# One column sum for the variance of two layer norms, and two transposed groups in the small PSUM ring, in a two-layer decoder trunk

## The chip, the cores and the metric

One core of a Trainium2 chip runs the whole kernel in one launch. The metric is the device time of that launch in microseconds (us), as the median of several executions.

## The reference, cut to what matters

The input is one sequence of 512 positions with 1024 features. Two layers follow each other. Layer 0 mixes with a state-space group and a stick-breaking attention group, layer 1 with a gated causal convolution of width 31 that has a layer norm of its own. Each layer adds its mixer to the scaled residual, normalises, adds a squared-ReLU MLP of width 4096, and normalises again:

```python
def layer_norm(x, g, b):
    mu = jnp.mean(xf, axis=-1, keepdims=True)
    var = jnp.mean(jnp.square(xf - mu), axis=-1, keepdims=True)
    y = (xf - mu) * lax.rsqrt(var + LN_EPS)
    return y * g + b

for layer in range(2):
    mix = ... if layer % 2 == 0 else conformer_conv(x, ...)
    x = layer_norm(DEEPNORM_ALPHA * x + mix, ln1_g[layer], ln1_b[layer])
    ffn = jnp.square(jax.nn.relu(x @ w1 + b1)) @ w2 + b2
    x = layer_norm(DEEPNORM_ALPHA * x + ffn, ln2_g[layer], ln2_b[layer])
```

So there are four layer norms between the stages and one inside the convolution. The kernel calls them a (after the mixer of layer 0), b (after the MLP of layer 0), c (inside the convolution), d (after the mixer of layer 1), and the last one, which works on another layout.

## The kernel before

**Layout.** Activations stand with features on the 128 partitions and positions along the free dimension: eight tiles X[0] to X[7] of 128 features by 512 positions. A matrix product in full precision is made of three products of rounded parts: a number is split into a high part (`whi`, `xh`, `hh`, `ah`) by ScalarE and the rest (`wlo`, `xl`, `hl`, `al`) by VectorE, and TensorE adds high by high, high by low and low by high into one PSUM bank (`gemm`, L257).

**Layer norm in this layout.** The mean over the features is a sum over the partitions, so it is a product on TensorE with a constant matrix `ones` that holds 1/1024. It runs for each half of the positions (256 columns) apart. `LN.add` keeps a running sum of the eight tiles on VectorE, and `LN.colmean` makes the mean of it with one product (the tile `mp`). `LN.centre` then subtracts the mean from each of the eight tiles on VectorE and squares each on ScalarE (the tiles `sq`), and adds the squares in four pairs on VectorE. It returns four tiles, and `LN.scale` makes the variance with four products that add into one bank (the tile `vp`), all on line L955. After that ScalarE takes an inverse root, VectorE refines it (the helpers on L386 and L390), and `ln_to_x` scales each tile and splits it into high and low parts for the next stage. The intermediate tiles of 128x512 come from a ring `tmp` of eight.

**What covers a layer norm.** TensorE works its queue in order. `tail_norm_lead` puts the last product of a stage and the first product of the next around each norm: `Tail.run(n)` makes n output tiles of the stage that ends (`tlb`, `tld`: 24 matmuls of 256 columns each), `Lead.run(n)` makes n tiles of the next stage for the first half of the positions (`pl` for the convolution's input, `fl` for the MLP of layer 1). `BEFORE = (1, 3, 1, 2)` says how many of them stand before the mean and before the variance of the first half, and of the second half. `issue_after` ties the norm's products behind them. For norm b the lead holds four tiles, of which one is left after the variance of the second half; for norm d it holds six, of which three are left.

**PSUM.** After the mixer two rings share the eight banks: `nps` with six (the tag "n"), and `stp` with two (the tag "st"), which the norms' products use, and later the MLP of layer 1 for its hidden tiles.

**The residual of layer 1.** The MLP of layer 1 makes its output with positions on the partitions, so `residual()` scales X and turns it: 32 transposes of 128x128 on TensorE, in eight groups of four, each group into one bank (`xt`, L1343), and each bank copied back to X by ScalarE (L1346). All eight groups took `nps` banks. At that point six tiles of the lead `fl` hold the six banks of the ring until ScalarE has taken their ReLU (the tile `r`), in `pair`, which also squares them and makes their sums and splits (`q`, `ah`, `al`, L1363 and L1364). After the residual `seven` starts the second product (`s`, L1397), whose banks come from the same ring.

**Order.** Within these bounds a planner orders the instructions of each engine when the program is built: the one that was written first goes first, and another goes ahead where by the planner's own clock the first is not ready yet. On the chip each engine then keeps its list in that order. For the convolution alone the order on TensorE, VectorE and ScalarE is written out by hand (`CONV_ORDER`).

Of the kernel before, what the change touches and what calls it, by code (L numbers as in the profile page):

```python
# [13 lines left out]
ALU = mybir.AluOpType  # L14
# [29 lines left out]
LEAD = 6  # L44
TOGETHER = {'fl1': 2}
LN_ON_V = "abcd"
KEEP_FROM = 8
AHEAD = (5, 4)
FJ = 3
# [110 lines left out]
def units_of(name, w, k0, nk, cols, width):  # L160

    ncol = 1024 // nk
    out = []
    for c in cols:
        base = c // width * width
        src = w[k0 * P : (k0 + nk) * P, base : base + width].rearrange("(k p) n -> p k n", p=P)
        out.append(((name, k0, base), src, nk, ncol, c - base, width))
    return out
# [29 lines left out]
def kernel(ctx: ExitStack, tc: tile.TileContext, a: dict, out: bass.AP):  # L198
# [42 lines left out]
    def pv(n, i):  # L241
        if n == "mix_b_in":
            return PB[:, i : i + 1]
        return PV[:, vrow[n] + i : vrow[n] + i + 1]
# [67 lines left out]
    with tc.high_priority():  # L312
        for j in range(KT):
            tag, bufs = (("spt", MIX_BUFS[3]), ("wt", MIX_BUFS[4]), ("q", QK_BUFS[0]), ("k", QK_BUFS[1]))[(0, 1, 0, 1, 0, 1, 3, 2)[j]]
            xt = att.tile([P, 4, P], F32, tag=tag, name=f"xin{j}", bufs=bufs)
# [69 lines left out]
    def tt(o, x, y, op):  # L385
        V.tensor_tensor(o, x, y, op=op)  # L386
        return o
# [244 lines left out]
    def in_proj(tile_i, name):  # L632
        w = W.next()
        ps = mm(name)
        proj_last[:] = [gemm(ps, w, slice(0, P), xs, 0, T)]
        return ps, pv("mix_b_in", tile_i)

    Ud = [tc.dram_tile([P, T], F32, name=f"Ud{j}") for j in range(4)]
    for j in range(4):
        ps, b = in_proj(j, f"u{j}") if j else (u0, pv("mix_b_in", 0))  # L640
# [231 lines left out]
    def nps(name):  # L872
        return nps_.tile([P, T], F32, tag="n", name=name)
# [7 lines left out]
    def tmp(name, dt=F32):  # L881
        return hid.tile([P, T], dt, tag="tmp", name=name, bufs=8)
# [14 lines left out]
    for layer in range(2):  # L897
# [4 lines left out]
        for nb in FFN_BLOCKS[layer]:  # L902
# [11 lines left out]
            for m in range(k0, k0 + nb, 4):  # L914
                units += units_of("f10", a["ffn_w1"][0], 0, 8, range(m * P, min(m + 4, k0 + nb) * P, 128), 256)
                if m >= KEEP_FROM:
                    keep_at["f", m + 3] = kept[n : n + 2]
# [14 lines left out]
    class LN:  # L932
# [29 lines left out]
        def centre(self, ys, c0, c1, other=None):  # L962

            mu = self.colmean([self.s[c0]], c0, c1, "m", other)
            sq = []
            for j, y in enumerate(ys):
                tt(y[:, c0:c1], y[:, c0:c1], mu, ALU.subtract)
                sq.append(tmp(f"sq{self.n}{c0}{j}")[:, c0:c1])
                act(sq[j], y[:, c0:c1], AF.Square)
            for j in range(0, KT, 2):  # L970
                tt(sq[j], sq[j], sq[j + 1], ALU.add)
            return sq[::2]

        def scale(self, sq, c0, c1, other=None):
            var = self.colmean(sq, c0, c1, "v", other)
# [360 lines left out]
    def residual():  # L1336
        for j in range(KT):
            act(X[j], X[j], AF.Identity, bias=rb[3][:, j : j + 1], scale=ALPHA)
        for f in range(2):
            pss = [nps(f"xt{b}{f}") for b in range(4)]  # L1340
            for b in range(4):
                for i in range(4):
                    PE.transpose(pss[b][:, i * P : (i + 1) * P], X[4 * f + i][:, b * P : (b + 1) * P], ident)  # L1343
            for b in range(4):
                XT[2 * b + f] = X[4 * f + b]
                S.copy(X[4 * f + b], pss[b])  # L1346
# [64 lines left out]
    for bi, nb in enumerate(FFN_BLOCKS[1][:-1]):  # L1411
        if bi:
            W.load_quads(k0, a["ffn_w2"][1], k0, nb)
        As = [pair(m, first[m : m + 2] if bi == 0 else None) for m in range(k0, k0 + nb, 2)]
        if bi == 0:
            residual()
        seven(k0, As, bi == 0)
        k0 += nb
# [26 lines left out]
    pss = [nps(f"h{b}0") for b in range(4)]  # L1445
# [66 lines left out]
```

## Time and profile before

| | |
|---|---|
| median of 3 runs | 1172.3 us (1169.31 to 1175.33) |
| the profiled execution | 1168.87 us, of which the span from first to last instruction is 1167.2 us |
| TensorE busy in the span | 1137.1 us (97%), mean granted clock 0.997 |
| VectorE, ScalarE, GpSimd busy | 816.3 us (70%), 550.0 us (47%), 66.2 us (6%) |
| DMA | 169.59 MB, mean 145 GB/s |

The rows that follow in the prediction come from views of this one execution. In a row of the timeline stand the start and the length in us, the engine, the line, the operation, the output and the inputs, the shape and how many were merged; in brackets the engine's idle time ahead of it and what ended that. A row of the chain of waits has start, length, engine, tile and line. Matmuls overlap: their listed length is longer than the distance from one to the next, so distances between starts are used. One matmul of plain f32 numbers, as on L955, shows as two records, each with its own weight load; the rows count the records.

### The profile page before, as it was taken

Reading aid. Unit: us, or ns where it says so; the run is one execution under the profiler, and the core shown is the slowest. Engines: PE = TensorE matmul, PEld = TensorE weight load, DVE = VectorE, ACT = ScalarE, POOL = GpSimd, SP = SyncE. Lnnn points to the kernel's source line nnn. Section 1 sums busy time; section 2 is a strip of 40 time slices with the busy share of each in tenths; the row PEclk is TensorE's granted clock in tenths of the full one; section 3 lists DMA queues with packets and bytes.
Section 4 is the critical chain, followed back from the end, with each engine's and each line's share of the span. In section 5 each row is a group of like instructions: output and inputs, shape, how many; then the busy total and the mean of one; then the engine's idle time right before and its main releaser. Section 6 shows DMA issues by size and latency. Waiting matters only on the chain.

```text
span 1167.2 us, 17873 instructions
## 1 busy us (share of the span) xinstructions
PE 1137.1 (97%) x7180; PEld 952.1 (82%) x7180; DVE 816.3 (70%) x1389; ACT 550.0 (47%) x838; POOL 66.2 (6%) x125
## 2 busy tenths in 40 slices
PE   9989999999999999999999999899999999999997
PEld 7777777799888888888899877589988888888885
DVE  7999875498645545645647699987595958688337
ACT  6857779345525424424413132463663536263530
POOL 1021211000000000000011211002000000000000
PEclk9999999999999999999999999999999999999999
DMA  8621221242687877888435743246024151515211
GB/s 204 167 66 50 72 69 62 90 146 69 225 286 254 284 275 270 270 281 276 147 116 174 252 143 112 72 149 216 1 82 136 38 161 45 170 30 162 63 54 72
DMA packets 145907, 169.59 MB, mean 145 GB/s; under 512 B 13922, under 2 KB 119138, under 8 KB 145824
## 3 DMA queue, kind: packets, MB, share of 16 engines
q1 hardware_dynamic: 137024, 136.96, 37.1%
q0 software_dynamic: 8640, 31.46, 8.0%
q8 instruction: 56, 0.92, 0.3%
q14 instruction: 27, 0.22, 0.1%
q10 hardware_dynamic: 160, 0.03, 0.0%
HBM read 132.12 MB, written 35.65 MB: 144 GB/s over the span
## 4 chain that ended last, share of the span: by engine, by line
PE 78%; ACT 4%; DMA 3%; DVE 2%; issue 1%; POOL 0%; SPq 0%; DVEq 0%; ACTq 0%
PE f L257 21%; PE acf L257 10%; PE s L1397 10%; PE fl L257 5%; PE tld L257 4%; PE h L1442 4%; PE tlb L257 4%; PE pv L257 3%; DMA raw<-in_ffn_w_dram 3%; PE pg L257 3%; PE cw L1171 3%; PE tla L257 2%; PE acmo L257 2%; PE pl L257 2%; PE gg L257 1%
## 5 line engine op out<-in xcount | busy, mean ns | idle before, releaser
L111 ACT CAST whi<-raw 128x1024 fp32r<-128x1024 f32 (+1 forms) x150 | 156.7, 1061 | 259.9 <-PE acf L257 67.3
L112 DVE TENSOR_TENSOR wlo<-raw,whi 128x1024 fp32r<-128x1024 f32 (+1 forms) x150 | 183.7, 1238 | 122.9 <-ACT whi L111 120.6
L257 PE MATMUL f<-xah,whi 128*128 128x512 f32 x208 | 81.0, 390 | 0.0
L257 PE MATMUL f<-xal,whi 128*128 128x512 f32 x208 | 81.0, 389 | 0.0
L257 PE MATMUL f<-xah,wlo 128*128 128x512 f32 x208 | 80.9, 389 | 0.0
L257 PE MATMUL f<-xdh,whi 128*128 128x512 f32 x208 | 80.9, 389 | 0.0
L257 PE MATMUL f<-xdl,whi 128*128 128x512 f32 x208 | 80.9, 389 | 0.0
L257 PE MATMUL f<-xdh,wlo 128*128 128x512 f32 x208 | 80.9, 389 | 0.0
L257 PE MATMUL acf<-hh,wlo 128*128 128x512 f32 x192 | 75.7, 394 | 0.0
L257 PE MATMUL acf<-hl,whi 128*128 128x512 f32 x192 | 75.7, 394 | 0.0
L257 PE MATMUL acf<-hh,whi 128*128 128x512 f32 x192 | 75.3, 392 | 0.0
L1397 PE MATMUL s<-whi,ah 128*128 128x512 f32 x168 | 64.6, 392 | 0.6 <-ACT X L1346 0.6
L1397 PE MATMUL s<-whi,al 128*128 128x512 f32 x168 | 65.0, 390 | 0.0
L1397 PE MATMUL s<-wlo,ah 128*128 128x512 f32 x168 | 64.9, 389 | 0.0
L112 DVE TENSOR_TENSOR wlo<-quad,whi 128x1536 fp32r<-128x1536 f32 x28 | 49.2, 1756 | 8.6 <-ACT whi L111 8.5
L390 DVE SCALAR_TENSOR_TENSOR cy<-hp,wdw,cy 128x512 f32<-128x512 f32 (+1 forms) x75 | 49.6, 661 | 1.3 <-ACT cy L186 1.3
L111 ACT CAST whi<-quad 128x1536 fp32r<-128x1536 f32 x28 | 41.1, 1478 | 19.4 <-PE s L1397 9.5
L96 POOL DMA_DIRECT2D whi<-kepth x30 | 16.0, 535 | 551.8 <-PE tlb L257 388.3
L257 PEld LDWEIGHTS f<-xdh,wlo 128*128 128x128 f32 x208 | 39.0, 188 | 8.2
L257 PEld LDWEIGHTS f<-xal,whi 128*128 128x128 f32 x208 | 39.0, 188 | 8.1
L257 PEld LDWEIGHTS f<-xah,wlo 128*128 128x128 f32 x208 | 39.0, 188 | 8.1
L257 PEld LDWEIGHTS f<-xdl,whi 128*128 128x128 f32 x208 | 39.0, 188 | 8.1
(647 smaller groups left out, 3061.4 us busy)
## 6 DMA issues: line engine op xcount, KB each, us to landing
raw<-in_ffn_w_dram SPq DMA_DIRECT2D x35, 1024.0 KB, 5.6
kepth<-whi SPq DMA_DIRECT2D x30, 512.0 KB, 3.9
keptl<-wlo SPq DMA_DIRECT2D x30, 512.0 KB, 9.4
whi<-kepth POOLq DMA_DIRECT2D x30, 512.0 KB, 3.5
wlo<-keptl POOLq DMA_DIRECT2D x30, 512.0 KB, 4.6
raw<-in_ffn_w_dram SPq DMA_DIRECT2D x28, 512.0 KB, 4.1
raw<-in_conv_w_pw_dram SPq DMA_DIRECT2D x12, 1024.0 KB, 7.4
quad<-in_ffn_w_dram SPq DMA_DIRECT2D x16, 768.0 KB, 4.5
```

The costliest lines, as they stand in the source:

```text
L96: nc.gpsimd.dma_start(x, d)
L111: i0 = nc.scalar.copy(hi, raw).ins
L112: i1 = nc.vector.tensor_sub(lo, raw, hi.bitcast(F32)).ins
L257: ins = PE.matmul(ps[:, c0:c1], u[:, k, ksl], v[:, c0:c1], start=start and k == 0 and i == 0, stop=stop and k == n - 1 and i == 2).ins
L390: V.scalar_tensor_tensor(o, x, s, y, op0=op0, op1=op1)
L1171: PE.matmul(cps[j, c0][g][C, :], Ds[j][t // 16][R, t % 16, :], hps[j][R, t + c0 : t + c1], start=t < 4, stop=t >= n - 4, tile_position=(R. ...
L1397: PE.matmul(ps, u, v[:, p, :], start=chain == i and p == 0 and n_ == 0, stop=p == len(As) - 1 and n_ == 2, skip_group_check=True)
L1442: PE.matmul(ps, u, v, start=k == 0 and i == 0, stop=k == nb_last - 1 and i == 2)
```

## The change

For the norms b and d the four pair sums of squares are added up to one tile on VectorE, so the variance takes one product with `ones` where it took four. For the residual, two of the eight transposed groups (the first two of the second four, `xt01` and `xt11`) take their banks from the small ring `stp`.

```diff
+ONE_SUM = "bd"
...
             for j in range(0, KT, 2):
                 tt(sq[j], sq[j], sq[j + 1], ALU.add)
-            return sq[::2]
+                if self.n in ONE_SUM and j:
+                    tt(sq[0], sq[0], sq[j], ALU.add)
+            return sq[:1] if self.n in ONE_SUM else sq[::2]
...
         for f in range(2):
-            pss = [nps(f"xt{b}{f}") for b in range(4)]
+            pss = [(stp if f and b < 2 else nps)(f"xt{b}{f}") for b in range(4)]
```

`scale` calls `colmean`, which makes one product for each tile that it is given.

## Prediction

> **What bounds the kernel now.** I read the page first, then the chain of waits, then the busy time by stretches, and last the timelines of TensorE (PE), VectorE (DVE) and ScalarE (ACT) around the two norms and the residual.
>
> ```profile
> span 1167.2 us, 17873 instructions
> PE 1137.1 (97%) x7180; PEld 952.1 (82%) x7180; DVE 816.3 (70%) x1389; ACT 550.0 (47%) x838; POOL 66.2 (6%) x125
> ```
> ```profile
> 595.00:642.00 47.00, 46.86 (x377) 46.13 (x376) 30.83 (x79) 14.72 (x35) 8.60 (x16) 1.00 0.54 180
> 790.00:835.00 45.00, 45.00 (x361) 44.47 (x360) 30.86 (x82) 17.89 (x42) 6.33 (x12) 1.00 0.42 141
> 852.80:860.50 7.70, 5.98 (x43) 4.90 (x42) 7.70 (x10) 7.70 (x15) 0.00 (x0) 1.00 0.00 0
> ```
> ```profile
> 610.42 1.73 PE vpb L955 x8
> ...
> 632.61 1.74 PE vpb L955 x8
> ...
> 803.11 1.73 PE vpd L955 x8
> ...
> 825.41 1.73 PE vpd L955 x8
> ...
> 850.79 1.04 ACT ah L1363
> ...
> 858.20 0.49 ACT X L1346
> 858.74 28.91 PE s L1397 x126
> ```
>
> TensorE is busy for 97% of the span, and the stretches (columns: length, PE, weight loads, DVE, ACT, GpSimd, clock, DMA share, GB/s) show it full through norm b (46.86 of 47.00 us) and norm d (45.00 of 45.00). All four variance products lie on the chain of waits at 1.73 us each. The residual is another kind of place: there DVE and ACT have work for all of the 7.70 us, TensorE for 5.98, and the chain runs through ACT from 850.79 until the product `s` starts. What shortens TensorE's queue in the norms is therefore gained one for one. What shortens it at the residual is gained only as far as ACT and DVE let the next product start.
>
> **Part 1: three products fewer in each of four places.** The price of one comes from the mean, which is the very form that remains (one product, two records), beside the variance (eight records), in the first half of norm b:
>
> ```profile
> 601.14 0.28 PE L257 MATMUL tlb<-hh,wlo 128*128 128x256 f32 x1
> 601.27 0.59 PE L955 MATMUL mpb<-sb,ones 128*128 128x256 f32 x2
> ...
> 601.81 0.28 PE L257 MATMUL tlb<-hl,whi 128*128 128x256 f32 x1
> ...
> 610.14 0.28 PE L257 MATMUL tlb<-hh,wlo 128*128 128x256 f32 x1
> 610.26 1.89 PE L955 MATMUL vpb<-sqb,ones 128*128 128x256 f32 x8
> ...
> 612.10 0.28 PE L257 MATMUL tlb<-hl,whi 128*128 128x256 f32 x1
> ```
>
> Between the two plain matmuls around the mean lie 601.81 - 601.14 = 0.67 us, around the variance 612.10 - 610.14 = 1.96. Both gaps hold the same two plain distances, so they cancel: the difference, 1.96 - 0.67 = 1.29 us, is what six records fewer are worth. Four places give 4 x 1.29 = 5.16 us, if the one product that is left is not late.
>
> **Part 2: three more sums in front of that product.** It needs all eight squares, through a chain on DVE that had four independent sums and gets seven, three of which read the sum just before.
>
> ```profile
> 604.55 1.43 DVE L386 TENSOR_TENSOR sqb<-sqb,sqb 128x256 f32<-128x256 f32 x4
> ...
> 629.56 1.43 DVE L386 TENSOR_TENSOR sqb<-sqb,sqb 128x256 f32<-128x256 f32 x4
> ...
> 635.35 0.42 DVE L386 TENSOR_TENSOR tb<-tb,rb 128x256 f32<-128x256 f32 x1
> 635.80 0.42 DVE L390 SCALAR_TENSOR_TENSOR rb<-tb,rb 128x256 f32<-128x256 f32 x1
> ...
> 753.96 1.43 DVE L386 TENSOR_TENSOR sqc<-sqc,sqc 128x256 f32<-128x256 f32 x4
> ...
> 822.35 1.42 DVE L386 TENSOR_TENSOR sqd<-sqd,sqd 128x256 f32<-128x256 f32 x4
> ```
> ```profile
> 632.45 1.89 PE L955 MATMUL vpb<-sqb,ones 128*128 128x256 f32 x8
> ...
> 754.44 1.99 PE L955 MATMUL vpc<-sqc,ones 128*128 128x256 f32 x8 [0.31 <-DVE sqc L386]
> ...
> 825.25 1.89 PE L955 MATMUL vpd<-sqd,ones 128*128 128x256 f32 x8
> ```
>
> Four independent sums take 1.43 us, the last of them 0.42, so they start (1.43 - 0.42) / 3 = 0.34 apart. A DVE operation that reads its forerunner's result starts 635.80 - 635.35 = 0.45 after it. Seven sums in the order of the code take 3 x 0.34 + 3 x 0.45 + 0.42 = 2.79, which is 1.36 us more than now. The way from DVE to a waiting product is seen at norm c: the first sum ends at 753.96 + 0.42 = 754.38, the product starts at 754.44, so 0.06.
>
> First half of b: the sums end at 604.55 + 1.43 + 1.36 = 607.34, the product's turn comes at 610.26. The cover is the three `tlb` tiles ahead of it, with 2.9 us to spare. DVE's queue behind the sums drains further `tlb` tiles from a ring of six banks; it is 1.36 us later and catches up in the idle time there. The first half of d has the same order and nearly the same cover. Both are costed at nothing.
>
> Second half of b: 629.56 + 2.79 + 0.06 = 632.41 against a turn at 632.45. Second half of d: 822.35 + 2.79 + 0.06 = 825.20 against 825.25. That is a tie to within 0.05 us. The product's weight load belongs to it and starts about one plain distance (0.12) ahead, so I take 0.1 us lost at each, 0.2 in all. Behind the waiting product stand the lead tiles, so a delay here is paid by TensorE in full. The bounds: 0 (sums at the independent distance, 0.34, end 0.33 earlier) and 1.29 for each, where the gain is eaten up, which takes another 1.3 us on DVE, the length of one weight split there.
>
> The Trainium skill, page "VectorE: DVE Perf Modes", section "The DRAIN you can't avoid", says that the pipe is flushed after every DVE operation and that chaining cost the same with and without a semaphore after each. By it the dependent sums would cost no more than independent ones, 0.34 each, and the sum of this change would be 0.2 us better. The trace differs: 0.45 against 0.34. The measurement decides.
>
> After the product, the inverse root and the scaling move up with it. Norm b's second half then has one lead tile of cover left and norm d's three, as now, so TensorE and the vector work both shift by the same 1.29.
>
> **Part 3: the residual.**
>
> ```profile
> 852.88 2.34 PE L1343 MATMUL xt<-ident,X 128*128 128x128 f32 x20
> 856.04 1.14 PE L1343 MATMUL xt<-ident,X 128*128 128x128 f32 x8 [0.81 <-ACT r L186]
> 857.52 0.66 PE L1343 MATMUL xt<-ident,X 128*128 128x128 f32 x4 [0.34 <-ACT X L1346]
> 858.74 0.50 PE L1397 MATMUL s<-whi,ah 128*128 128x512 f32 x1 [0.56 <-ACT X L1346]
> ...
> 860.47 0.40 PE L1397 MATMUL s<-whi,al 128*128 128x512 f32 x1
> ```
> ```profile
> 855.32 0.67 ACT L186 ACTIVATE r<-fl,PV 128x512 f32<-128x512 f32 x1
> 855.89 0.57 ACT L1346 COPY X<-xt 128x512 f32<-128x512 f32 x1
> ...
> 857.35 0.85 ACT L1363 CAST ah<-q 128x768 fp32r<-128x768 f32 x1
> 858.09 3.04 ACT L1346 COPY X<-xt 128x512 f32<-128x512 f32 x6
> ```
> ```profile
> 857.59 1.75 DVE L134 TENSOR_TENSOR quad<-quad,quad 128x1536 f32<-128x1536 f32 x1
> 859.26 0.95 DVE L1364 TENSOR_TENSOR al<-q,ah 128x768 fp32r<-128x768 f32 x1
> ```
>
> Five groups (20 transposes) run at once; the sixth waits 0.81 us for the last ReLU, the eighth 0.34 and `s` 0.56 for copies: 1.71 us idle. With two groups in the small ring, seven groups run at once: 28 x 0.115 = 3.2 us, until 856.1. The eighth takes the sixth bank of the large ring, free from 855.99, and ends about 856.6. The first `s` tile then takes the bank of the first copy (done at 856.46) and starts near 856.6, two microseconds earlier. But its matmuls come in the order of the three pairs of hidden tiles, three to a pair. The eighth (pair 3, low part) is the row at 860.47, and the low part `al` that it reads ends on DVE at 859.26 + 0.95 = 860.21. DVE has no gap ahead of it (a subtraction on the quadrants runs from 857.59), and ACT made its `ah` only by 858.20. So `s` does six matmuls (1.4 us), stands until 860.27, and is then 860.47 - 860.27 = 0.2 us ahead of now. The idle time moves and does not go away; late next is the split of the third pair.
>
> Bounds: at best the start of `s` counts in full, 858.74 - 856.6 = 2.1 us, if the planner puts `al` or the pair's sums earlier, since its clock sees `s` ready sooner. At worst three of the copies, now ready sooner, slip ahead of the pair's work on ACT, at 0.5 us each (3.04 / 6): 1.5 lost. I take 0.2, as the order of ACT and DVE up to this split hangs on nothing that the change frees. No other queue is passed: the change adds no DMA, and the small ring's last reader is norm d, 20 us before.
>
> **The sum.** 5.16 - 0.2 + 0.2 = 5.2 us. The profiled execution would go from 1168.87 to 1163.7 (span 1162.0). It ran 3.4 us under the median of the runs, 1172.3; on the median the sum gives 1167.1 us, 0.44% less.
>
> **The rivals.**
>
> (a) The residual pays nearly in full: 5.0 + 1.9 = 6.9 us, 1165.4. For it: 1.71 us of idle time do stand on TensorE. Against it: the row at 859.26.
>
> (b) The variance products of the second halves are late by 1.3 us each and those two places gain nothing: 2 x 1.29 + 0.2 = 2.8, 1169.5. For it: a margin of 0.05 us. Against it: DVE does nothing else there; behind the sums it is idle until the root.
>
> (c) A stall for instructions moves.
>
> ```profile
> q8 instruction: 56, 0.92, 0.3%
> ```
> ```profile
> 745.25 1.41 PE L1171 MATMUL cw<-hp,D 32*32 32x256 f32 x55 [2.69 <-issue]
> ```
>
> TensorE's 7180 + 7180 records over 56 loads are 256 for each. In the densest stretch of the convolution's taps it waits 2.69 us for nothing but issue. Six products fewer ahead of it (24 records) move the borders of these loads by a tenth of one. The stall can vanish or come twice: 1164.4 or 1169.8. Against it: 24 records are few beside that dense stretch, so a border should still fall in it.
> The Trainium skill, page "Runtime: NRT & Kernel Launch", section "Instruction fetch mechanics", holds that crossing such a border is mostly hidden. By it this rival would be worth nothing; the row with 2.69 us says otherwise.
>
> (d) Slower than before: the planner's clock shifts at norm b, and a weight load of layer 1 goes out behind another.
>
> ```profile
> raw<-in_ffn_w_dram SPq DMA_DIRECT2D x35, 1024.0 KB, 5.6
> ```
>
> One such load exposed, with its split on DVE (at least the 0.95 us of the smaller one above) costs 6.5 us, gives 1172.3 - 5.2 + 6.5 = 1173.6, and decides from 5.2 on. Against it: TensorE stands full in both norms, and no part of the change touches a load.
>
> **How the numbers follow.** Forecast 0.52, (a) 0.18, (b) 0.10, (c) 0.12, (d) 0.08. About 0.5% (5.9 us, a time of 1166.4) is what a measurement of this kernel can tell from no change; the forecast lies 0.7 us on the near side of it, and the three runs spread over 6 us, so I let 0.4 of it count as faster: 0.21, with most of (a) 0.15 and half of (c) 0.06 it makes 0.42. Slower by that much: half of (d) and runs of (b) and (c) at their worst, 0.07. The rest, 0.51, is within. The range, 1163.0 to 1171.0, holds (a), (b) and both ends of (c); (d) is left out, and some of the spread.
>
> **What would show it.** Right: `vpb` and `vpd` with four records each instead of sixteen, their turn taking about 0.43 us; DVE sums of squares with 14 to a norm instead of 8; the second halves' products with a wait of 0 to 0.2 us on DVE; at the residual 28 transposes without a break, and the eighth matmul of `s` waiting for `al`. Wrong: a wait of over 0.5 us in a second half, an `s` stretch that starts its stream 1 us or more earlier against the last `fl` tile, an issue stall that is not near 2.7 us, or a wait for `wlo` after norm b.

## The result, and the profile after

| | before | after | ratio, 95% interval |
|---|---|---|---|
| median of 6 runs each, us | 1171.74 (1167.37 to 1175.33) | 1161.31 (1158.74 to 1164.90) | 0.9927 [0.9903, 0.9952] |
| the same again, later, us | 1170.93 | 1163.87 (1160.82 to 1166.92) | 0.9941 [0.9920, 0.9961] |
| profiled execution, us | 1168.87 | 1164.90 | |

The change is faster by 0.6 to 0.7%. The forecast was 0.44%. The median of 1161.3 lies under the lower end of the range, 1163.0; the ratio, applied to the median the prediction started from, gives 0.9927 x 1172.3 = 1163.7, just inside. Both ratios are faster than the 0.5% that the prediction called telling, an outcome to which it gave 0.42 against 0.51 for a time within it.

First the page of the changed kernel, the span and the line of the engines (columns as in the prediction):

```profile
span 1163.2 us, 17835 instructions
PE 1133.7 (97%) x7156; PEld 948.5 (82%) x7156; DVE 820.6 (71%) x1401; ACT 550.0 (47%) x838; POOL 70.2 (6%) x125
```

TensorE has 24 matmul records fewer, DVE 12 more: twelve products of two records each and twelve sums, as the diff says. But the two spans differ by only 4.0 us, less than the runs do. GpSimd's busy time went from 66.2 to 70.2, and the change has nothing there. The timelines of GpSimd, before and after, name the place, in the attention stage some 450 us ahead of the first changed instruction:

```profile
156.04 0.50 POOL L705 TENSOR_SCALAR_AFFINE_SELECT w2B<-w2B 128x256 f32<-128x256 f32 x1 [4.41 <-ACT w2B L192]
```
```profile
154.67 4.04 POOL L706 TENSOR_SCALAR_AFFINE_SELECT w2B<-w2B 128x256 f32<-128x256 f32 x1 [4.42 <-ACT w2B L193]
```

The same select took 0.50 us in one execution and 4.04 in the other, and norm b's first mean started 3.5 us later (604.73 against 601.27). So two whole executions can't be subtracted here. What can be compared is the stages around the change, from the first matmul of one to the first matmul of the next; where the code is the same, these repeat within about 0.1 us from execution to execution (`pv` stands for the first of the unbroken run of `pv` matmuls):

| stage, us | before | after | difference |
|---|---|---|---|
| norm b: first mean to `pv` | 47.96 | 45.51 | -2.45 |
| norm d: first mean to `xt` | 59.00 | 56.40 | -2.60 |
| residual: `xt` to the first `f` | 34.60 | 32.36 | -2.24 |
| sum | | | -7.29 |

7.29 us are 0.62% of 1170, which agrees with both ratios. Other stages do not repeat so well. The one from the first tap `cw` to norm c's first mean takes 78.8 to 80.5 us in the executions of this and the kernels below, with no order that the edits would explain. The four longest, 80.1 to 80.5 in e3, e4, e7 and e8, are those in which TensorE's granted clock stood at 0.50 for 3.41 us inside it; the last section says more on that.

Busy time by stretches (columns as before), norm b and the residual of the changed kernel:

```profile
598.46:643.01 44.55, 44.29 (x365) 43.87 (x364) 32.74 (x85) 14.77 (x35) 8.61 (x16) 1.00 0.56 190
851.10:858.80 7.70, 7.70 (x52) 6.74 (x51) 7.70 (x10) 7.70 (x15) 0.00 (x0) 1.00 0.00 0
```

Norm b is still full but for 0.26 us. The residual's 7.70 us, in which TensorE had worked for 5.98, are now full. The second halves of norms b and d on TensorE and DVE:

```profile
634.63 0.28 PE L258 MATMUL pl<-xbh,whi 128*128 128x256 f32 x1
634.75 0.59 PE L956 MATMUL vpb<-sqb,ones 128*128 128x256 f32 x2
...
638.35 0.74 PE L258 MATMUL pl<-xbh,whi 128*128 128x256 f32 x4 [0.26 <-ACT xbh L187]
...
824.76 0.28 PE L258 MATMUL fl<-xdh,whi 128*128 128x256 f32 x1
824.88 0.59 PE L956 MATMUL vpd<-sqd,ones 128*128 128x256 f32 x2
```
```profile
631.74 2.55 DVE L387 TENSOR_TENSOR sqb<-sqb,sqb 128x256 f32<-128x256 f32 x7
...
821.87 2.55 DVE L387 TENSOR_TENSOR sqd<-sqd,sqd 128x256 f32<-128x256 f32 x7
```

One product stands where four stood, with no wait in brackets ahead of it. The sums ended at 631.74 + 2.55 = 634.29, and the product started 0.46 later.

The residual, on TensorE, ACT and DVE:

```profile
851.10 3.81 PE L1346 MATMUL xt<-ident,X 128*128 128x128 f32 x32
854.74 0.49 PE L1400 MATMUL s<-whi,ah 128*128 128x512 f32 x1
...
856.22 0.40 PE L1400 MATMUL s<-whi,ah 128*128 128x512 f32 x1
856.46 0.40 PE L1400 MATMUL s<-whi,al 128*128 128x512 f32 x1
856.69 0.39 PE L1400 MATMUL s<-whi,ah 128*128 128x512 f32 x1
```
```profile
855.57 0.86 ACT L1366 CAST ah<-q 128x768 fp32r<-128x768 f32 x1
856.30 3.05 ACT L1349 COPY X<-xt 128x512 f32<-128x512 f32 x6
```
```profile
855.81 1.75 DVE L135 TENSOR_TENSOR quad<-quad,quad 128x1536 f32<-128x1536 f32 x1
857.48 0.95 DVE L1367 TENSOR_TENSOR al<-q,ah 128x768 fp32r<-128x768 f32 x1
```

All 32 transposes run in one go, and `s` starts 3.64 us after the first of them instead of 5.86. DVE and ACT do what they did, at the same distance from the first transpose: `al` starts 857.48 - 851.10 = 6.38 us behind it, before 859.26 - 852.88 = 6.38. The low part is ready only at 858.43, yet TensorE does not stand: the matmuls come through every 0.23 us.

### The profile page after: what moved, and what is told of

It is laid out like the page before. It is cut to its first block, busy times and chain, and to the rows that moved or that the text cites. A ratio compares the mean times of both kernels' runs of the same rounds, so it can differ in the third digit from the quotient of the medians.

```text
span 1163.2 us, 17835 instructions
## 1 busy us (share of the span) xinstructions
PE 1133.7 (97%) x7156; PEld 948.5 (82%) x7156; DVE 820.6 (71%) x1401; ACT 550.0 (47%) x838; POOL 70.2 (6%) x125
## 4 chain that ended last, share of the span: by engine, by line
PE 78%; DMA 6%; DVE 6%; ACT 5%; issue 2%; SPq 2%; POOL 1%; DVEq 0%; ACTq 0%
PE f L258 20%; PE acf L258 10%; PE s L1400 10%; DMA raw<-in_ffn_w_dram 4%; PE tld L258 4%; PE h L1445 4%; PE tlb L258 4%; PE fl L258 3%; PE pv L258 3%; PE cw L1174 3%; PE pg L258 3%; PE tla L258 2%; PE acmo L258 2%; DVE wlo L113 2%; PE pl L258 2%
## 5 line engine op out<-in xcount | busy, mean ns | idle before, releaser
L258 PEld LDWEIGHTS f<-xdh,whi 128*128 128x128 f32 x208 | 39.0, 188 | 8.1
L258 PEld LDWEIGHTS f<-xah,whi 128*128 128x128 f32 x208 | 39.0, 188 | 8.1
```

What stands on the lines that cost most here:

```text
L258: ins = PE.matmul(ps[:, c0:c1], u[:, k, ksl], v[:, c0:c1], start=start and k == 0 and i == 0, stop=stop and k == n - 1 and i == 2).ins
```

## The experiments

Three questions were open: where the 2.24 us of the residual come from, whether the variance products were as close to late as the prediction said, and whether norms a and c would pay too. The stages of every kernel, in us (each ratio is against runs of the kernel before made beside it, whose medians lie between 1167.7 and 1171.7, so ratios can be compared down the table and times cannot):

| | norm b | norm d | `xt` to `s` | `xt` to `f` | time, us (runs) | ratio to before |
|---|---|---|---|---|---|---|
| before | 47.96 | 59.00 | 5.85 | 34.60 | | |
| after | 45.51 | 56.40 | 3.63 | 32.36 | 1161.31 (6) | 0.9927 [0.9903, 0.9952] |
| e1_ring | 47.97 | 59.00 | 3.63 | 32.36 | 1169.23 (12) | 0.9992 [0.9976, 1.0008] |
| e2_sums | 45.52 | 56.40 | 5.86 | 34.56 | 1163.34 (7) | 0.9948 [0.9930, 0.9967] |
| e3_ring_order | 45.52 | 56.40 | 3.63 | 36.10 | 1163.23 (12) | 0.9951 [0.9934, 0.9967] |
| e4_order | 45.50 | 56.40 | 5.85 | 34.55 | 1170.09 (1) | |
| e5_abd | 45.50 | 56.40 | 3.63 | 32.36 | 1162.38 (5) | 0.9955 [0.9941, 0.9969] |
| e6_abcd | 45.51 | 54.13 | 3.64 | 32.38 | 1165.10 (11) | 0.9971 [0.9959, 0.9983] |
| e7_late | 46.71 | 56.40 | 3.63 | 32.33 | 1164.00 (1) | |
| e8_al_first | 45.50 | 56.40 | 3.63 | 33.74 | 1161.57 (1) | |
| e9_bd_c2 | 45.51 | 54.12 | 3.64 | 32.34 | 1160.51 (6) | 0.9922 [0.9894, 0.9950] |

In e6 and e9 the column of norm d can't be read alone: the first mean of d stands later among the other matmuls there, and from c's first mean to d's it takes 45.66 and 44.64 us instead of 43.30.

**e1_ring: the ring alone**, the sums as before.

```
-            pss = [nps(f"xt{b}{f}") for b in range(4)]
+            pss = [(stp if f and b < 2 else nps)(f"xt{b}{f}") for b in range(4)]
```


> The kernel before with the two transposed groups in the small ring alone; the norms make four variance products as before. The list of TensorE differs from before only in the first s block: the third pair's low-part products stand behind the other tile's first six and the next weight's first three. Stage measure: from the first transpose to the first f matmul behind the first s block (34.8 us before, 32.5 after). Theory 1 (the ring frees the start, and the re-sorted list keeps s running until the split of the third pair is there): 32.5, the run 2.2 us faster, about 0.2%. Rival (the ring alone is worth the 0.2 us that was predicted, and the rest of the change's gain at this place comes from the shift by the norms): 34.5, no change of the run.

The stage is 32.36 us, the changed kernel's to 0.01, so the 2.24 us belong to the ring alone and need no sums. The timed runs, at 0.9 us faster with an interval from 2.8 faster to 0.9 slower, hold 2.24 but can't tell it from nothing. TensorE's waits, by what ended them (columns: sum, times, longest):

```profile
PE cw L1171 <- issue: 1.9, 1, 1.9
```

This kernel removes no records ahead of `cw` and has 1.9 us there, the changed kernel 2.3, before 3.1: more below.

**e2_sums: the sums alone**, the residual in the old ring.

```
-            pss = [(stp if f and b < 2 else nps)(f"xt{b}{f}") for b in range(4)]
+            pss = [nps(f"xt{b}{f}") for b in range(4)]
```


> The changed kernel with the residual's eight groups back in the large ring: the one variance product in norms b and d alone. Theory 1: 1.2 to 1.3 us at each of the four places, 5.0 us in all (0.43%), residual stage 34.8 us as before. The wait for instructions in the dense stretch of taps, 2.7 us before and 1.7 after, stays at 1.7 if it is the 24 records ahead of it that moved it. Rival (the products of the second halves are late): 2.6 us, with a wait on DVE in the rows of the second halves.

Norms b and d gain what they gain in the changed kernel (2.44 and 2.60), the residual nothing. The parts add: 5.08 with what the residual varies by, and 2.24, against 7.29 together. The wait for issue in `cw`, expected at 1.7 us, was 2.6. The old wait at the residual stands where it stood:

```profile
PE xt L1346 <- ACT r L187: 0.8, 1, 0.8
```

**e3_ring_order: the changed kernel with `s` tied to the order of the code.** TensorE's queue in the first `s` block differs between before and after, though the code doesn't (`sXYZ` is one tile, `pN` its three matmuls with the Nth pair):

```
before  s010 p0, p1, p2            s011 p0, p1, p2 ...
after   s010 p0, p1                s011 p0 ...         whi.ah of p2 among them;
        the products with al of p2 behind the next weight's first ones
```

The planner sorts by the times it forecasts, and with `s` ready sooner it put others ahead of the pair that is late. e3 takes that away and leaves the ring:

```
-        bank = {}
+        bank, tied = {}, []
...
+                        if first and i in (1, 2):
+                            if tied:
+                                tc.add_manual_dep(ins, tied[-1], NOSYNC, reason="order as written")
+                            tied.append(ins.name)
```


> The changed kernel with the first two weights' products of the first s block tied in the order in which they are written, which is the order before. Theory 1 (the re-sorted list pays): the transposes still run without a break and s starts about 3.6 us after the first of them, but its eighth matmul waits about 1.5 us for the third pair's low part; stage 34.3 to 34.6 us, the run 1.8 to 2.0 us slower than the changed kernel and so 0.45% faster than before. Rival (the ring alone pays, the list is without weight): stage 32.5, as fast as the changed kernel.

TensorE around the third pair, the split that it waits for, and then the stretches from the first transpose on:

```profile
856.86 0.50 PE L1400 MATMUL s<-whi,ah 128*128 128x512 f32 x1
858.87 0.50 PE L1400 MATMUL s<-whi,al 128*128 128x512 f32 x1 [1.51 <-DVE al L1367]
...
860.25 0.63 PE L1400 MATMUL s<-whi,ah 128*128 128x512 f32 x1
860.67 0.63 PE L1400 MATMUL s<-whi,al 128*128 128x512 f32 x1
```
```profile
857.86 0.95 DVE L1367 TENSOR_TENSOR al<-q,ah 128x768 fp32r<-128x768 f32 x1
```
```profile
851.49:855.12 3.63, 3.63 (x34) 3.40 (x33) 3.63 (x4) 3.63 (x7) 0.00 (x0) 1.00 0.00 0
855.12:860.00 4.88, 3.29 (x14) 2.19 (x13) 4.88 (x7) 4.88 (x10) 0.00 (x0) 1.00 0.00 0
860.00:863.40 3.40, 3.40 (x10) 2.63 (x9) 3.40 (x4) 2.88 (x4) 0.00 (x0) 0.50 0.01 2
863.40:887.59 24.19, 24.19 (x109) 20.00 (x107) 16.65 (x18) 7.76 (x8) 0.00 (x0) 1.00 0.59 177
```

The eighth matmul waits for `al` and starts 858.87 - 851.49 = 7.38 us behind the first transpose; before it was 860.47 - 852.88 = 7.59. So in the order of the code the ring is worth 0.21 us up to there, which is the prediction's 0.2 with its mechanism. In this execution it is then worth less than nothing: in the seventh column, TensorE's clock, stands 0.50 for 3.40 us, from 1.1 us behind the wait's end on, the matmuls come every 0.42 us instead of 0.23, and the stage takes 36.10, which is 1.50 more than before and 3.74 more than with the planner's order. Those slow matmuls cost about 1.6 us by their distances (nine of them take 3.64 us instead of 2.05). Without them the stage would be about 34.5, as it was before and as was expected for this run. So against the planner's order the written one loses by its wait in any case; the slow clock behind it is what this one execution met, and the last section shows that it hangs on where the wait lies. The timed runs of e3 and e2 (1163.23 and 1163.34) do not show the 1.5 us; at intervals of some 2 us to each side they could not.

**e4_order: that order alone, by hand, in the old ring** (with the sums).

```
+            steps = [(t, p) for t in range(2) for p in range(len(As))]
+            if first and i == 1:
+                steps = [(t, p) for t in range(2) for p in range(2)] + [(0, 2), (1, 2)]
```


> The one-sum norms, the residual in the large ring as before, and only the order of the first s block changed by hand: the third pair's products behind the first six of both tiles. Theory 1 (ring and order pay only together): s cannot start before the copy that frees its bank, the idle time of 1.7 us stays, stage 34.6 to 34.8 us. Rival (the order alone keeps TensorE fed): under 33.5 us.

The stage is 34.55 us, as without it. `s` still starts 5.85 us behind the first transpose. In the order of the code the first product with the third pair's `al` came 7.59 us behind that transpose before, when the split is done (`al` ends at 7.33), so another order had no wait there to fill. The waits are the old ones:

```profile
PE xt L1346 <- ACT r L187: 0.8, 1, 0.8
PE s L1400 <- ACT X L1349: 0.6, 1, 0.6
```

Neither the early start (e3) nor the order pays alone; together they pay 2.24. The one timed run, 1170.09, is no shorter than before's although norms b and d gain their 5.1 here too: this execution reached the first mean of norm a 255.8 us after its start, 6.6 later than before's, with nothing changed up to there.

**e8_al_first: e3 with the third pair's split ahead of the subtraction on DVE**, so that `al` comes sooner and the order of the code stays.

```
+            late = sub(b11, b22, b11).ins
+            if blk == 0:
+                self.tc.add_manual_dep(late, self.al, NOSYNC, reason="behind the third pair's split")
```


> The ring with the tied order of the run before, and on VectorE the third pair's split ahead of the subtraction on the quadrants. Theory 1 (with that order s waits for the split, and the slower matmuls behind the wait come from the wait of 2 us): the split ends about 6.4 us after the first transpose, the eighth matmul of s starts at 6.4 instead of 7.4, the matmuls behind it keep their distance of 0.23 us, stage 33.2 to 33.6 us. Rival (the slower matmuls have another cause than the length of the wait): distance 0.43 us for some three microseconds again, 35 us or more.

```profile
853.02 0.50 PE L1404 MATMUL s<-whi,al 128*128 128x512 f32 x1 [0.76 <-DVE al L1369]
```

The wait falls from 1.51 to 0.76 us, the clock stays at 1.00, and the stage takes 33.74, 2.36 less than e3, some 1.6 of it by the clock, and slightly over what was expected. What is left against the planner's order, 1.38, lies in the distances around this wait: 1.26 us from the matmul ahead of it to the one that waits, instead of 0.23, another 0.25 ahead of that, for `ah`, and 0.1 behind it.

**e7_late: three idle DVE operations more behind the sums of the second halves of b and d**, to see how near the product is to being late. They compare a sum with itself and change no value.

```
+            if self.n in ONE_SUM and c0:
+                for _ in range(3):
+                    tt(sq[0], sq[0], sq[0], ALU.max)
```


> The changed kernel with three idle operations more on VectorE (a maximum of the tile with itself) behind the sums in the second halves of b and d, 1.4 us: the list of TensorE then has the product ten matmuls of the lead later. Theory 1 (the product itself never waits, since the planner moves lead matmuls ahead of it; what counts is the cover that is left behind it, one lead tile at b and three at d): norm b, from its first mean to the convolution's first tile, 46.7 to 47.0 us (45.5 with the change), norm d 56.4 as with the change. Rival (the margin of 0.05 us at the product is what counts): both 1.2 to 1.4 us longer.

```profile
631.33 1.35 DVE L387 TENSOR_TENSOR sqb<-sqb 128x256 f32<-128x256 f32 x3
```
```profile
PE pl L258 <- ACT xbh L187: 1.5, 1, 1.5
```

In both norms the product goes 1.2 us later (7.50 us behind its mean instead of 6.30) without waiting for a moment: the planner puts more lead matmuls ahead of it. Norm b then loses 1.20 us, because its lead tiles run out and the next ones wait 1.5 us for `xbh`, where they had waited 0.26. Norm d, with three tiles of lead, loses nothing.

**e5_abd: norm a with one sum too.**

```
-ONE_SUM = "bd"
+ONE_SUM = "abd"
```


> The changed kernel with norm a too on one sum of squares. Theory 1 (wherever TensorE is full and the planner finds other products for the time of the sums, the product is what is saved): 1.2 to 1.3 us in each half of norm a, 2.5 us more than the change, 0.84 to 0.88% faster than before. Rival (in norm a VectorE also splits weights, the sums come late and the product waits): 0 to 1 us.

Norm a, from its first mean to `acf`, takes 61.26 us instead of 59.87 (59.77 to 59.89 in the executions that leave norm a alone): it loses 1.4 where two halves of 1.29 were to be had, and where even the rival had expected no loss. The waits say why; the changed kernel has no such row.

```profile
PE fl L258 <- ACT xah L187: 3.5, 2, 2.1
```

Each half has a wait for its own scaled input. The product, its root and the scaling come 1.1 us of sums later, norm a has too little lead behind its product to cover that, and the waits take more than the products gave.

**e6_abcd: all four norms.**

```
-ONE_SUM = "bd"
+ONE_SUM = "abcd"
```


> Norms a, b, c and d on one sum of squares; norm c stands in the convolution, whose order is written by hand, and there the four products start one after the other as the pair sums come (0.31 us wait on VectorE before). Theory 1: in the first half of c the one product waits for the last sum, about 1.3 us later than now, with nothing to run in between, so some 0.5 to 1 us is lost there; in the second half 1.3 us are gained: between 0.3 and 0.8 us over the kernel with a, b and d. Stage from the mean of c to the mean of d 43.3 us before, 42.5 to 43.0 here. Rival (the four products are simply replaced, as in b and d): 40.7.

Norms c and d together, from c's first mean to `xt`, take 99.79 us, in the changed kernel 99.70: c gains nothing. Its second half gains (e9 below), its first half loses as much: the product there waits for the seventh sum, and the clock halves behind that wait, in the taps. How much of the loss is the wait and how much the clock, one execution doesn't tell.

```profile
PE vpc L956 <- DVE sqc L387: 2.8, 1, 2.8
```
```profile
755.00:758.00 3.00, 3.00 (x78) 1.90 (x80) 2.74 (x7) 2.97 (x7) 0.00 (x0) 0.50 0.25 90
```

The timed runs are 3.4 us faster than before (2.0 to 4.8), while the stages of the profiled execution add up to 5.8: 1.4 lost in a, 2.45, 2.53 and 2.22 gained in b, in c and d, and at the residual. The profiled execution is the fastest of the eleven runs, 3.8 us under their median. What the other runs lost is not shown.

**e9_bd_c2: b, d and the second half of c.**

```
-                if self.n in ONE_SUM and j:
+                if self.n in ONE_SUM + "c" * (c0 > 0) and j:
```


> The changed kernel with one sum of squares also in the second half of norm c, where tiles of the next product stand around the variance; its first half keeps four products. Theory 1 (one sum pays where other products fill the time of the sums and of the root behind it, as in b and d): 1.2 to 1.3 us over the change, from the mean of c to the residual 98.4 us (99.7 with the change and before). Rival (the root behind the product comes late for the next product, as in norm a, where one sum lost 1.4 us): 99.7 or more.

From c's first mean to `xt` it takes 98.76 us, 0.94 less than the changed kernel, a little under what one place gives elsewhere and under the 1.2 to 1.3 that were expected. At a ratio of 0.9922 it is the fastest version tried; its lead of 0.9 us over the changed kernel is told by the stage, not by the timed runs.

**after_again: the changed kernel once more.**

> The changed kernel on the same chip as the run beside it, as its yardstick: 0.62% faster than before by the stages (7.3 of 1170 us), norms b and d and the residual with the stage times seen.

The three stages are the same to 0.02 us (45.52, 56.40, 32.34). The wait for issue in `cw` is 2.0 us, where the first execution of the same code had 2.3.

## Why the prediction was right, and where it was wrong

**Part 1, right.** 1.29 us were forecast for each of four places. First half of b 1.29, second half 1.17, first half of d 1.30, second half 1.30: together, before rounding, 5.05 against 5.16. The second half of b misses 0.12, which stands in the row with 0.26 for `xbh`; the prediction had named that norm's one tile of cover.

**Part 2, right in its sum, wrong in its margin.** The seven sums were to take 2.79 us and the products of the second halves to lose 0.1 each to a tie. The sums took 2.55, because only the last of them followed right behind the sum it reads (0.44 us apart, the others 0.34), and the planner put one lead matmul more ahead of the product (6.30 us behind its mean instead of 6.18). So there was no wait, and rival (b) did not come true. e7 shows what sets the price: not the tie at the product, which the planner moves, but the cover behind it. Norm b has none left for 1.35 us more, norm d has, and norm a had none for the sums themselves.

**Part 3, wrong.** The term was 0.2 us, and 2.24 were measured. The step that failed is "its matmuls come in the order of the three pairs of hidden tiles": TensorE's queue was re-sorted. All else in the step held: `al` came at the same distance to 0.01 us, ACT and DVE kept their order, and in the order of the code the eighth matmul was 0.21 ahead (e3). An `s` that starts 1 us or more earlier was one of the prediction's own signs of being wrong, and it started 2.2 earlier. I had let the planner's clock move ACT's and DVE's work within the bounds, and not the work of the very engine whose start was moved. Rival (a), with its bound of 2.1 for the residual, was the right size: 5.05 + 2.24 = 7.3, where (a) said 6.9. The mechanism was another, though: nothing waited for came sooner; TensorE had other work in the meantime.

The prediction also held that in the written order the idle time "moves and does not go away". In e3 that is so, with 1.59 us idle instead of 1.71; but in one piece it can cost more: the three pauses before, of 0.81, 0.34 and 0.56 us, had left the clock at 1.00, and behind the single one it halved.

**Rival (c), not shown.** The waits for issue in `cw` were 3.1 us before, 2.3 and 2.0 in two executions of the changed kernel, and 1.9 to 3.2 in the others, 1.9 in e1 with not one record fewer ahead of `cw`. That spread, and e1's place in it, leave nothing that could be put down to the 24 records. An issue stall that is not near 2.7 us was a sign of being wrong as well; the longest went from 2.7 to 1.7, and by the same spread that says nothing about the change. What sets these waits stays open. **Rival (d)** did not come: no load of weights was exposed.

In all: 5.05 of the 7.29 us came from where the prediction had put them, 2.24 from a step it had priced at a tenth of that, and the timed 0.6 to 0.7% hold the sum. That the time still falls inside the range is no merit of part 3: the range had been drawn wide enough for rival (a).

## What to carry to other kernels

Where a planner orders an engine's queue, a start that comes sooner is not priced by the next operand that is late: ask first what else that engine could do until then, and whether the planner would put it there. Trading products on TensorE for sums on VectorE pays the full price of the products while independent matmuls cover the whole way from the sums to the scaled input, and loses more than it gave where they don't; count that cover for each place, not for the kernel. When single executions differ by a few us ahead of the edit, compare the stages, and look whether the clock stood at full speed in each before you call their difference the edit's.

## What the runs showed of the hardware

A wait of TensorE can cost more than its length. Behind the 1.51 us in e3 and the 2.8 us in e6 the granted clock stood at 0.50. Length alone doesn't decide: in e5 TensorE waited 2.06 us for `xah`, and the clock stayed at 1.00:

```profile
279.76 0.86 PE L258 MATMUL fl<-xah,whi 128*128 128x256 f32 x5 [2.06 <-ACT xah L187]
```

Where the wait lies decides too. In every trace the stretches at 0.50, but for one that runs through the end of the execution, last 3.41 us or two or three times that, and they start whole multiples of 3.413 us apart. In e3 they start at 85.15, 160.24, 747.34 and 859.97 us, and the distances are 22, 172 and 33 times 3.413. So time can be cut into pieces of 3.413 us on a grid that each trace shows for itself. The first rows are e3's, the last two pieces of them with the wait and behind it; then e5's two pieces around its wait; then the changed kernel's piece with the wait behind the long select that is told below:

```profile
85.15:88.56 3.41, 3.41 (x14) 3.02 (x13) 2.20 (x4) 1.06 (x2) 0.14 (x1) 0.50 0.09 23
160.24:167.06 6.82, 5.99 (x20) 3.73 (x20) 0.54 (x1) 3.18 (x7) 0.29 (x1) 0.50 0.00 0
747.34:750.75 3.41, 3.41 (x73) 1.65 (x72) 2.43 (x6) 1.94 (x6) 0.00 (x0) 0.50 0.01 2
856.55:859.97 3.42, 1.83 (x7) 1.12 (x7) 3.42 (x4) 3.42 (x8) 0.00 (x0) 1.00 0.00 0
859.97:863.38 3.41, 3.41 (x10) 2.64 (x9) 3.41 (x4) 2.89 (x4) 0.00 (x0) 0.50 0.01 2
```
```profile
275.33:278.74 3.41, 2.37 (x19) 2.11 (x17) 1.71 (x5) 0.47 (x1) 0.00 (x0) 1.00 0.00 0
278.74:282.15 3.41, 2.39 (x19) 2.39 (x20) 3.41 (x9) 1.88 (x5) 0.00 (x0) 1.00 0.00 0
```
```profile
155.98:159.39 3.41, 0.00 (x0) 0.00 (x0) 3.23 (x5) 0.00 (x0) 3.41 (x2) 1.00 0.46 146
159.39:166.21 6.82, 5.93 (x15) 2.85 (x16) 0.00 (x0) 2.01 (x5) 0.30 (x2) 0.50 0.02 6
```

The wait of e3 lies whole in one piece, which has 1.59 us idle, and the next piece runs at 0.50. A border cuts the longer wait of e5 into 1.04 and 1.02 us, and nothing happens. The residual before had its three pauses cut into 0.81 and 0.90 us by a border at 856.78. Between 90 and 1150 us of all twelve traces, 12 pieces at full clock have 1.9 us or more idle, and each of the 12 is followed by 0.50; of 11 with 1.5 to 1.9 us, 2 are; of 3680 with less, 1 is, in e4. What tells those cases in between apart, and the one in e4, stays open. So the same code can meet the slow clock in one execution and miss it in the next: the changed kernel has such a stretch at 84.3 us in its first execution, and none there in its second.

The Trainium skill, page "TensorE: Matmul & The Clock Gate", section "What's actually happening", gives a window of 3413 ns that runs freely; the traces agree, with the multiples of 3.413 us above and a grid that lies differently in each. Its table in "Why this matters for your kernels" warns of gaps over about 3 us; e3 and e6 show shorter ones, of 1.51 and 2.8 us. The same page holds in "Part 4: PE-mode transpose" that transposes don't count as busy in the same way, and e3's wait does come behind 32 of them; but `s` takes over from them 1.4 us ahead of the piece that holds the wait, and no run here shows that they had a part in it.

The GpSimd select of 0.50 us took 4.02 to 4.06 us in both profiled executions of the changed kernel and in those of e1, e3 and e4, and 0.48 to 0.52 in the seven others. Nothing that was changed lies ahead of it. What TensorE waited for `w2C`, the next tile in GpSimd's queue, went from 2.1 to 5.2 us (before, and the changed kernel):

```profile
PE av L756 <- POOL w2C L705: 2.1, 2, 1.2
```
```profile
PE av L757 <- POOL w2C L706: 5.2, 2, 4.4
```

Behind that wait the clock stands at 0.50 for 6.8 us, as the rows above show. The five executions with the long select reach norm a's first mean after 252.8 to 255.8 us, the seven others after 248.0 to 251.1. What makes the select long stays open. With the clock it is a good part of why the profiled executions differ ahead of the edit, and likely of why the timed runs of one kernel spread by some 6 us.
